# Starting a latent gather in the layer before: rows of the first layer's expert tables fetched during the context's second layer

## The chip, the cores and the metric

The kernel runs on one core of a Trainium2 chip. The metric is the time of one execution in device microseconds. The engines are named as in the profile: PE is the matrix engine (TensorE), DVE the vector engine (VectorE), ACT the scalar engine (ScalarE), POOL the GpSimd engine, SP the queue that issues most loads and stores.

## What is computed

One inference step of a two-layer trunk for two token streams: 128 context tokens (modulated, reading only themselves) and 512 latent tokens (reading the context too). Each layer is a mixer of three branches and then an expert layer (PEER):

```python
x <- LayerNorm(alpha*x + gate1 * W_out( sum_b sigmoid(g_b(h)) * P_b(mixer_b(h)) ))   # gated scan, convolution, attention
x <- LayerNorm(alpha*x + gate2 * PEER(h))
```

```python
q = (xf @ w_pq).reshape(nt, PEER_HEADS, 2, PEER_DQ // 2)
s = jnp.einsum('thpc,hpkc->thpk', q, keys)
s1, i1 = lax.top_k(s[:, :, 0], PEER_TOPK)
s2, i2 = lax.top_k(s[:, :, 1], PEER_TOPK)
...
top_s, top_pos = lax.top_k(cand, PEER_TOPK)
eidx = jnp.take_along_axis(cidx, top_pos, axis=-1)
gate = jax.nn.softmax(top_s, axis=-1)
...
act = jax.nn.gelu(jnp.einsum('td,thkd->thk', xb, u_tab[ib]), approximate=False)
return jnp.einsum('thk,thkd->td', gb * act, v_tab[ib])
```

There are 8 heads of 16 chosen experts, so 128 chosen rows of `u_tab` and 128 of `v_tab` for each token, out of 16384 rows of 1024 numbers each.

## The kernel before

Work is in tiles of 128 tokens: one for the context, four for the latents. The expert layer is done in two ways. For a tile that is **gathered** (the context's one tile, and tile 0 of the latents, in each layer), `peer_gather` fetches for each of the 128 choices one row per token by an indirect DMA on the POOL queue (128 rows of 4 KB, 0.5 MB, into a buffer `grow`), and DVE works it in: a product summed into `gw` for a row of the u table (`gjunk`, L922), and a multiply-add into `gacc` for a row of the v table (L934). After each 16 u rows ACT takes a Gelu of 16 columns. That makes 256 rows a tile. For the other three latent tiles the layer is **dense**: PE multiplies all 128 blocks of 128 experts by the tokens. `u_hidden` loads a block of the u table, splits it on ACT and DVE into a high and a low part (`uH`, `uL`) and makes 24 matmuls of 128x384. Some of the blocks (108 of 128 in the first layer, 64 in the second: `AHEAD`) are done early by `u_ahead`, and their results are stored in DRAM (`sdr`). `gate_map` turns the routing into dense maps (`ob`, `oa`, `stage`, stored to `gdr`). In `peer_dense` each pair of blocks loads its part of the maps (`G`), loads or computes its hidden values (`da`), applies Gelu and map, splits them (`daH`, `daL`), and multiplies by two loaded blocks of the v table (`wraw`, split to `wh`, `wl`) into six accumulators (`acc`): 36 matmuls of 128x512.

The pieces run beside each other through generators. `bg_add(gen, rate)` registers one; each `tick()` in the foreground work advances every registered generator by its rate, and `bg_drain` runs it to its end. Within this program order, the framework's scheduler arranges each engine's queue by when it expects operands and buffers to be ready; a tile whose buffers are all held waits for one to be released. The rates are a hand-set table (`BG`, `RU`, `RG`): `BG[4]` is the rate of the latents' routing (`front`), `RU` that of `u_ahead`, `RG` that of the latents' gather.

The order in the first layer: the context's first layer and the latents' mixer (with the context's gather beside them); then the latents' normalisation, their routing in the background (`routing_keys`: eight projections by `w_pq`, then for each tile and head a score tile and the best 16; `routing_pairs`: the best 16 of the pairs, for four tiles), the second context layer in the foreground (`ctx_front(l + 1)`) and `u_ahead` in the background; then the gate maps of tiles 1 to 3, beside which the gather of tile 0 begins; then the dense stage with the rest of the gather at a rate worked out so that it ends ten ticks early. In the second layer there is no context work left, and the routing's pairs lie beside the gate maps.

Buffers that matter here: `x4`, four slots of 4 KB a partition with the tag `t4k`, which hold in turn the latents' `xlat`, the latents' `VV` and `SG` in the scan, and `uH` and `uL`. `grow` has five buffers in the gate stage and eight (shared with `wraw`) in the dense stage. In the context's scan (`gla_proj`, `gla_core`) `VV` and `SG` have buffers of their own, and `E`, the decay factors of one of seven levels, has two.

```python
    def t4k(shape, name, dt=F32, s=None, p=None):
        if s is not None and s.ctx:
            return p.tile(shape, dt, name=name, bufs=1)
        return x4.tile(shape, dt, tag="t4k", name=name)
```

Of the kernel before, what the change touches and what calls it, by code (L numbers as in the profile page):

```python
# [9 lines left out]
F32 = mybir.dt.float32  # L10
# [33 lines left out]
def kernel(ctx: ExitStack, tc: tile.TileContext, A: dict, O: list):  # L44
# [352 lines left out]
    def gla_proj(s, l, hH, hL, gp, setup, heads):  # L397

        a2, gb, gn, gaT, t4n = setup
        QK = gp.tile([128, 2, 4, 128], F32, name="QK", bufs=1 if s.ctx else 2)  # L400
        VV = t4k([128, 4, DV], "VV", F32, s, gp)
        SG = t4k([128, 4, DV], "SG", F32, s, gp)
        ZB = gp.tile([128, 2, 4, 128], F32, tag="t4", name="ZB", bufs=t4n)
# [24 lines left out]
    def gla_core(s, l, u, gp, t4n, QK, VV, SG, ZB):  # L428
# [25 lines left out]
        for li, m in enumerate(LEVELS):  # L454
            nb = 512 // (2 * m)
            E = gp.tile([128, 2, 512], F32, name="E", bufs=2)
            Ev = E.rearrange("p i (b h m) -> p i b h m", h=2, m=m)
# [332 lines left out]
    def routing_keys(s, l, hH, hL, vals, idxs, qp):  # L790

        for u in range(8):
            keys = qp.tile([128, 2, 128], F32, name="keys", bufs=2)
            nc.sync.dma_start(keys, A["keysT"][l, :, 2 * u:2 * u + 2, :])
            ps = proj_fm(s, hH, hL, w_for(s, A["w_pq"][l, u]))
            qs = []
            for f in range(2):
                q = qp.tile([128, s.T], F32, name="q", bufs=2)
                act(q, ps[f], AF.Copy)
                qs.append(q)  # L800
            for t in range(s.nt):
                p = pb([128, 2, 128])
                for f in range(2):
                    nc.tensor.matmul(p[:, f, :], qs[f][:, t * 128:(t + 1) * 128], keys[:, f, :], start=True, stop=True)
                sc = qp.tile([128, 2, 128], F32, name="sc", bufs=2)
                act(sc, p, AF.Copy)
                for f in range(2):
                    hp = 2 * u + f
                    top16(vals[t][:, hp, :], idxs[t][:, hp, :], sc[:, f, :])
                yield  # L810
# [342 lines left out]
    def run(gen):  # L1153
        for _ in gen:
            pass
# [98 lines left out]
    PL = (5, 5, 5, 2, 0)  # L1254
    BG = (0.55, 2.0, 2.8, 3.622, 0.8)
    FL = (0, 1, 0, 1)
# [3 lines left out]
    OB = ('APDAPADA', 'APDAPADA')  # L1260
    RG = (2.0, 1.056)
    RU = ((0.7, 1.0), (0.84, 0.8))
# [71 lines left out]
    for l in range(DEPTH):  # L1334
# [17 lines left out]
        with pool("e_lat") as ep:  # L1352
# [3 lines left out]
            more = l + 1 < DEPTH  # L1356

            def front(qp):
                yield from routing_keys(Lt, l, hH, hL, vals, idxs, qp)
                if more:  # L1360
                    for t in range(4):
                        yield from routing_pairs(t, vals, idxs, ep, qp, ro)

            ahead = pool("u_t6")
            ucfg.update(p=ahead.__enter__(), n=1, pool_l=PU[0])
            eu = bg_add(u_ahead(l, hH, hL), RU[l][0], PR[0])
            with w_pool(3, 2, PL[2]), pool("ro_lat", 2) as qp:
                with pool("ln_lat2") as lp:
                    run(ln_finish(Lt, 2 * l + 1, ln_rows(lp, 4), True))
                e = bg_add(front(qp), BG[4], PR[5])  # L1370
# [3 lines left out]
            ahead.__exit__(None, None, None)  # L1374
            gout = []
            ucfg["l"] = l
            with pool("g_lat") as gp, pool("u_lat") as up_:
                ucfg.update(p=up_, n=2, pool_l=PU[1 + l])
                with pool("gm") as qp:
# [7 lines left out]
                    pairs(0)  # L1387
                    e = bg_add(peer_gather(Lt, l, 0, ro[0][0], ro[0][1], gp, gout), RG[l], PR[1])
                    pairs(1)
# [6 lines left out]
                with pool("dense") as dp, w_pool(8, 3, PL[3 + l]):  # L1396
                    gcfg.update(p=wcfg["p"], tag="wraw", n=8, m=2)
                    e[1] = (256 + LAG - e[3]) / (256 - AHEAD[l] - 10)
                    peer_dense(Lt, l, hH, hL, dp, e, gout, gp)


# [109 lines left out]
```

## Time and profile before

| | |
|---|---|
| median of 3 runs | 5828.63 us (5822.93 to 5830.19) |
| the profiled execution | 5830.46 us, span 5828.7 us, clock 0.944 |
| busy PE, DVE, ACT, POOL | 89%, 74%, 35%, 46% of the span |
| mean DMA rate | 239 GB/s |

The span is the time from the first to the last instruction of the profiled execution. A busy share is a mean over stages with different limits. The granted clock is TensorE's: 1.00 stands for 2.4 GHz, 0.5 for 1.2 GHz.

### The profile page before, as it was taken

What the parts mean: (1) busy time and instruction counts of PE and PEld (TensorE: products, weight loads), DVE (VectorE), ACT (ScalarE), POOL (GpSimd) and SP (SyncE); (2) the same over time, 40 slices, a digit from 0 to 9 for tenths busy, and PEclk for the clock granted to TensorE, in tenths of its full rate; (3) what the DMA queues carried; (4) which work ended last, traced back from release to release, by engine and by line L of the source; (5) the groups of instructions that cost most, each with busy time, mean ns of one, the idle gap of its engine ahead of it and who ended that gap; (6) DMA issues with size and microseconds to landing.
All of it is one profiled execution on the core that took longest, in us unless ns stands there. A gap on an engine that the chain in (4) does not pass through costs nothing. (4 is left out here: it accounts for less than half of the span.)

```text
span 5828.7 us, 79381 instructions
## 1 busy us (share of the span) xinstructions
PE 5182.8 (89%) x28598; PEld 4504.3 (77%) x28598; DVE 4316.1 (74%) x7923; ACT 2048.9 (35%) x3446; POOL 2681.1 (46%) x2207
## 2 busy tenths in 40 slices
PE   7998799888899998899999787999989778899997
PEld 5887678767788898888777676777777778799876
DVE  3328878878554868887777788788778898777677
ACT  2213334221222125653333333333222356433333
POOL 1215544675210216775444455456752566444322
PEclk9999999999899999999999899999989889999999
DMA  7763356887556557889988533578852667888895
GB/s 279 268 237 114 109 191 220 302 290 255 203 208 240 191 205 270 314 326 321 319 305 312 193 112 125 188 259 296 280 181 93 231 235 258 290 273 278 278 315 207
DMA packets 456714, 1395.14 MB, mean 239 GB/s; under 512 B 42880, under 2 KB 184832, under 8 KB 413312
## 3 DMA queue, kind: packets, MB, share of 16 engines
q1 hardware_dynamic: 303248, 833.73, 40.2%
q0 software_dynamic: 153072, 556.34, 27.9%
q8 instruction: 225, 3.69, 0.2%
q14 instruction: 169, 1.38, 0.1%
HBM read 1275.29 MB, written 114.62 MB: 238 GB/s over the span
## 5 line engine op out<-in xcount | busy, mean ns | idle before, releaser
L917 POOL DMA_INDIRECT grow<-in_peer_v_dram,eidx x512 | 661.8, 1293 | 663.4 <-DVE gacc L934 291.6
L917 POOL DMA_INDIRECT grow<-in_peer_u_dram,eidx x512 | 666.4, 1302 | 567.4 <-DVE gjunk L922 198.3
L934 DVE SCALAR_TENSOR_TENSOR gacc<-grow,gw,gacc 128x1024 f32<-128x1024 f32 x508 | 689.0, 1356 | 91.3 <-DMA grow<-in_peer_v_dram,eidx 85.9
L922 DVE SCALAR_TENSOR_TENSOR gjunk<-grow,gh 128x1024 bf16<-128x1024 f32 x512 | 675.0, 1318 | 74.1 <-DMA grow<-in_peer_u_dram,eidx 65.9
L172 ACT ACTIVATE wh<-wraw 128x1024 fp32r<-128x1024 f32 (+1 forms) x388 | 515.3, 1343 | 540.7 <-PE pa L197 214.5
L174 DVE TENSOR_TENSOR wl<-wraw,wh 128x1408 fp32r<-128x1408 f32 (+2 forms) x388 | 565.9, 1461 | 177.1 <-ACT wh L172 175.6
L196 PE MATMUL acc<-wh,daH 128*128 128x512 f32 x1536 | 615.2, 401 | 60.4 <-ACT daH L110 46.3
L176 POOL TENSOR_TENSOR wl<-wraw,wh 128x640 fp32r<-128x640 f32 (+1 forms) x260 | 375.2, 1445 | 618.7 <-ACT wh L172 599.2
L198 PE MATMUL acc<-wh,daL 128*128 128x512 f32 x1536 | 614.4, 400 | 15.8 <-DVE daL L111 15.7
L197 PE MATMUL acc<-wl,daH 128*128 128x512 f32 x1536 | 610.7, 398 | 0.5 <-DVE wl L174 0.5
L196 PE MATMUL pa<-hH,wh 128*128 128x512 f32 x1312 | 544.3, 415 | 45.0 <-DVE th L746 12.3
L198 PE MATMUL pa<-hH,wl 128*128 128x512 f32 x1312 | 536.5, 410 | 11.7 <-DVE wl L174 11.5
L197 PE MATMUL pa<-hL,wh 128*128 128x512 f32 x1312 | 535.6, 408 | 0.7 <-DVE hL L111 0.7
L196 PE MATMUL po<-hH,uH 128*128 128x384 f32 x1376 | 492.3, 358 | 41.9 <-ACT uH L1014 20.0
L198 PE MATMUL po<-hH,uL 128*128 128x384 f32 x1376 | 478.3, 348 | 28.9 <-DVE uL L1016 28.8
L1014 ACT ACTIVATE uH<-uraw 128x1024 fp32r<-128x1024 f32 x256 | 270.6, 1057 | 590.6 <-PE po L197 201.5
L197 PE MATMUL po<-hL,uH 128*128 128x384 f32 x1376 | 476.1, 346 | 0.0
L196 PEld LDWEIGHTS acc<-wh,daH 128*128 128x128 f32 x1536 | 295.8, 193 | 131.5 <-ACT daH L110 58.4
L1016 DVE TENSOR_TENSOR uL<-uraw,uH 128x1024 fp32r<-128x1024 f32 (+1 forms) x256 | 290.9, 1136 | 115.2 <-ACT uH L1014 108.8
L198 PEld LDWEIGHTS acc<-wh,daL 128*128 128x128 f32 x1536 | 295.5, 192 | 94.1 <-DVE daL L111 32.2
L197 PEld LDWEIGHTS acc<-wl,daH 128*128 128x128 f32 x1536 | 296.4, 193 | 62.0 <-DVE wl L174 1.0
L1063 DVE TENSOR_TENSOR da<-da,G 128x384 f32<-128x384 f32 x256 | 184.1, 747 | 214.3 <-ACT da L1056 208.9
(367 smaller groups left out, 12228.2 us busy)
## 6 DMA issues: line engine op xcount, KB each, us to landing
wraw<-in_w_in_dram SPq DMA_DIRECT2D x168, 1024.0 KB
uraw<-in_u_T_dram SPq DMA_DIRECT2D x256, 512.0 KB
wraw<-in_v_n_dram SPq DMA_DIRECT2D x256, 512.0 KB
wraw<-in_w_mod_dram SPq DMA_DIRECT2D x48, 1024.0 KB
wraw<-in_w_branch_dram SPq DMA_DIRECT2D x48, 1024.0 KB
gdr<-stage SPq DMA_DIRECT2D x24, 2048.0 KB
G<-gdr SPq DMA_DIRECT2D x64, 768.0 KB
sdr<-ust SPq DMA_DIRECT2D x172, 192.0 KB
```

Of the source, the lines that this page charges most:

```text
L172: act(H, raw, AF.Copy)
L174: V.tensor_sub(L[:, :m], raw[:, :m], H[:, :m].bitcast(F32))
L176: nc.gpsimd.tensor_sub(L[:, m:], raw[:, m:], H[:, m:].bitcast(F32))
L196: nc.tensor.matmul(out, aH, bH, start=start, stop=False)
L197: nc.tensor.matmul(out, aH, bL, start=False, stop=False)
L198: nc.tensor.matmul(out, aL, bH, start=False, stop=stop)
L917: nc.gpsimd.indirect_dma_start(out=g, out_offset=None, in_=A[tab + str(l)], in_offset=bass.IndirectOffsetOnAxis(ap=eidx[:, j:j + 1], axis=0))
L922: pin(V.scalar_tensor_tensor(junk, g, 1.0, h, op0=OP.mult, op1=OP.mult, accum_out=w[:, j:j + 1]))
L934: pin(V.scalar_tensor_tensor(acc, g, w[:, j:j + 1], acc, op0=OP.mult, op1=OP.add))
L1014: act(uH, raw, AF.Copy)
L1016: V.tensor_sub(uL[:, :m, :], raw[:, :m, :], uH[:, :m, :].bitcast(F32))
L1063: V.tensor_mul(af, af, G[0][:, :, 2 * (i % 2) + f, :])
```

## The change

The gather of the first layer's tile 0 is registered as soon as that tile's routing is known, inside `front`, which runs beside the second context layer, at 1.6 rows a tick there; before, it was registered after the first call in the gate stage. In the gate stage its rate is 2.0 as before, and in the dense stage the rate is worked out from the rows that remain, as before. Its pool `g_lat` opens earlier, and a pool `g_rows` gives `grow` three buffers in the new place. The routing's rate `BG[4]` goes from 0.8 to 1.2.

Room for this comes from several tiles: in the second context layer `VV` and `SG` use the shared `t4k` slots; `E` has one buffer in both context layers; `keys` has one for the latents; the two `q` of a projection have one buffer each under names of their own (two before, in turn); in the first layer's routing `wh` and `wl` have one buffer and the normalisation's rows two instead of four.

```diff
-        VV = t4k([128, 4, DV], "VV", F32, s, gp)
-        SG = t4k([128, 4, DV], "SG", F32, s, gp)
+        room = None if l else s
+        VV = t4k([128, 4, DV], "VV", F32, room, gp)
+        SG = t4k([128, 4, DV], "SG", F32, room, gp)
...
-            E = gp.tile([128, 2, 512], F32, name="E", bufs=2)
+            E = gp.tile([128, 2, 512], F32, name="E", bufs=1 if s.ctx else 2)
...
-            keys = qp.tile([128, 2, 128], F32, name="keys", bufs=2)
+            keys = qp.tile([128, 2, 128], F32, name="keys", bufs=1 if s.nt > 1 else 2)
...
-                q = qp.tile([128, s.T], F32, name="q", bufs=2)
+                q = qp.tile([128, s.T], F32, name="q%d" % f, bufs=1)
...
-    BG = (0.55, 2.0, 2.8, 3.622, 0.8)
+    BG = (0.55, 2.0, 2.8, 3.622, 1.2)
...
-    RG = (2.0, 1.056)
+    RG = (2.0, 1.056, 1.6)
...
+            def gather(rate):
+                return bg_add(peer_gather(Lt, l, 0, ro[0][0], ro[0][1], gp, gout), rate, PR[1])
+
             def front(qp):
                 yield from routing_keys(Lt, l, hH, hL, vals, idxs, qp)
                 if more:
                     for t in range(4):
                         yield from routing_pairs(t, vals, idxs, ep, qp, ro)
-
+                        if not t:
+                            eg.append(gather(RG[2]))
+
+            eg = []
+            gpool = pool("g_lat")
+            rows = pool("g_rows")
+            if more:
+                gp = gpool.__enter__()
+                gcfg.update(p=rows.__enter__(), tag="grow", n=3, m=1)
...
-            with w_pool(3, 2, PL[2]), pool("ro_lat", 2) as qp:
+            with w_pool(3, 1 if more else 2, PL[2]), pool("ro_lat", 2) as qp:
                 with pool("ln_lat2") as lp:
-                    run(ln_finish(Lt, 2 * l + 1, ln_rows(lp, 4), True))
+                    run(ln_finish(Lt, 2 * l + 1, ln_rows(lp, 2 if more else 4), True))
...
-                    e = bg_add(peer_gather(Lt, l, 0, ro[0][0], ro[0][1], gp, gout), RG[l], PR[1])
+                    if more:
+                        e = eg[0]
+                        e[1] = RG[l]
+                    else:
+                        e = gather(RG[l])
```

Two places in the queues show what moves. The first is POOL in the second context layer, from the first tile's routing products (`oh`) to the first additions of a branch into `mg`. Before:

```order
L848 TENSOR_TENSOR oh<-oh,xf 128x256 x16
L748 TENSOR_TENSOR mg_14094<-mg_14094,th 128x128 x2
L848 TENSOR_TENSOR oh<-oh,xf 128x256 x4
L748 TENSOR_TENSOR mg_14095<-mg_14095,th 128x128 x2
L848 TENSOR_TENSOR oh<-oh,xf 128x256 x12
```

and now:

```order
L849 TENSOR_TENSOR oh<-oh,xf 128x256 x5
L918 DMA grow<-in_peer_u_dram,eidx 128x1024 x13
L575 MEMSET z 128x1
L576 MEMSET z 128x1
L918 DMA grow<-in_peer_u_dram,eidx 128x1024 x15
L849 TENSOR_TENSOR oh<-oh,xf 128x256 x16
L918 DMA grow<-in_peer_u_dram,eidx 128x1024 x4
L918 DMA grow<-in_peer_v_dram,eidx 128x1024 x16
L918 DMA grow<-in_peer_u_dram,eidx 128x1024 x6
L749 TENSOR_TENSOR mg_14363<-mg_14363,th 128x128 x2
L918 DMA grow<-in_peer_u_dram,eidx 128x1024 x7
L749 TENSOR_TENSOR mg_14364<-mg_14364,th 128x128 x2
```

The convolution's last `z`, the second tile's `oh` and the `mg` additions now stand behind gathers, 61 of them ahead of the second `mg`; before, none was among them.

The second place is DVE between the splits of the twenty-second and the twenty-third expert block of `u_ahead`. Before, the convolution stands there:

```order
L576 TENSOR_TENSOR z<-pa,cc 128x128
L579 SCALAR_TENSOR_TENSOR yc<-z,cw,yc 128x128
L580 SCALAR_TENSOR_TENSOR yc<-z,cw,yc 128x128
L576 TENSOR_TENSOR z<-pa,cc 128x128
L579 SCALAR_TENSOR_TENSOR yc<-z,cw,yc 128x128
L580 SCALAR_TENSOR_TENSOR yc<-z,cw,yc 128x128
L174 TENSOR_TENSOR wl<-wraw,wh 128x1408
L584 TENSOR_TENSOR yc<-yc,pa 128x128 x2
L1016 TENSOR_TENSOR uL<-uraw,uH 128x1024
```

and now, in part (the search of the second tile's pairs is `cand`, `top` and `pos`):

```order
L923 SCALAR_TENSOR_TENSOR gjunk,gw<-grow,gh 128x1024
L789 MAX_INDEX pos<-top,cand 128x8
L923 SCALAR_TENSOR_TENSOR gjunk,gw<-grow,gh 128x1024
L824 TENSOR_TENSOR cand<-vals_11287 128x128
L827 TENSOR_SCALAR cand<-vals_11287 128x8
L923 SCALAR_TENSOR_TENSOR gjunk,gw<-grow,gh 128x1024
L785 MAX top<-cand 128x8
L276 TENSOR_TENSOR mT<-pmod,bT 128x16
L786 MAX_INDEX pos<-top,cand 128x8
L277 TENSOR_SCALAR modT_95<-mT 128x16
L787 MATCH_REPLACE cand<-top,cand 128x136
L923 SCALAR_TENSOR_TENSOR gjunk,gw<-grow,gh 128x1024
```

Sixteen gathered rows stand between these two splits, with single small operations between them, and the last projection's `wl`, which stood here, has gone to just behind the seventeenth block.

## Rows read from the trace of the kernel before

**Rows 1.** Part 1 of the page: busy us, share, instructions.

```profile
PE 5182.8 (89%) x28598; PEld 4504.3 (77%) x28598; DVE 4316.1 (74%) x7923; ACT 2048.9 (35%) x3446; POOL 2681.1 (46%) x2207
```

**Rows 2.** Busy time by stretch: us, PE, PEld, DVE, ACT, POOL, PEclk, DMA share, GB/s.

```profile
900.00:1000.00 100.00, 98.52 (x584) 80.90 (x583) 86.68 (x151) 40.36 (x82) 51.20 (x45) 1.00 0.74 242
1496.00:1737.00 241.00, 228.50 (x1429) 197.40 (x1428) 120.20 (x438) 66.32 (x111) 40.42 (x40) 0.96 0.61 215
1737.00:1949.00 212.00, 204.25 (x1433) 183.96 (x1432) 108.64 (x473) 54.82 (x147) 24.98 (x30) 0.99 0.64 224
1949.00:2088.00 139.00, 120.15 (x807) 117.48 (x807) 117.25 (x406) 20.48 (x43) 47.65 (x69) 0.91 0.51 191
...
2204.00:2594.00 390.00, 344.72 (x2094) 336.03 (x2093) 334.32 (x477) 250.12 (x529) 292.65 (x210) 0.93 0.82 299
2594.00:2737.00 143.00, 140.73 (x698) 127.91 (x699) 118.59 (x121) 51.04 (x62) 95.50 (x80) 0.98 0.93 327
2737.00:3201.00 464.00, 422.92 (x1727) 335.51 (x1727) 339.37 (x398) 169.05 (x195) 196.68 (x203) 0.95 0.91 314
```

**Rows 3.** The same for PE's matmuls into `acc` alone: us, busy, PEclk, DMA share.

```profile
2737.00:3201.00 464.00, 422.92 (x1727) 0.95 0.91 314
...
5517.00:5549.00 32.00, 32.00 (x142) 1.00 0.95 325
5549.00:5772.00 223.00, 207.63 (x867) 0.97 0.90 310
```

**Rows 4.** The same for POOL's gather issues into `grow` alone.

```profile
1496.00:2204.00 708.00, 2.03 (x2) 0.97 0.61 214
2204.00:2594.00 390.00, 133.28 (x98) 0.93 0.82 299
...
2737.00:3201.00 464.00, 132.77 (x109) 0.95 0.91 314
3201.00:3272.00 71.00, 6.22 (x5) 0.98 0.60 207
...
5549.00:5772.00 223.00, 57.58 (x41) 0.97 0.90 310
```

**Rows 5.** Who waited for whom, 2700 to 3250: us, times, longest.

```profile
ACT da L1056 <- DMA da<-sdr: 308.4, 52, 11.3
...
PE acc L196 <- ACT daH L110: 33.4, 17, 5.0
```

**Rows 6.** The page's costliest groups: busy us, mean ns, idle before.

```profile
L934 DVE SCALAR_TENSOR_TENSOR gacc<-grow,gw,gacc 128x1024 f32<-128x1024 f32 x508 | 689.0, 1356 | 91.3 <-DMA grow<-in_peer_v_dram,eidx 85.9
L922 DVE SCALAR_TENSOR_TENSOR gjunk<-grow,gh 128x1024 bf16<-128x1024 f32 x512 | 675.0, 1318 | 74.1 <-DMA grow<-in_peer_u_dram,eidx 65.9
...
L1014 ACT ACTIVATE uH<-uraw 128x1024 fp32r<-128x1024 f32 x256 | 270.6, 1057 | 590.6 <-PE po L197 201.5
```

**Rows 7.** Line 917, POOL's gather issues: ns min, median, max.

```profile
L917 POOL DMA_INDIRECT grow<-in_peer_u_dram,eidx x512: 932/1099/2977, 554.9 to 5590.5; - x171
```

**Rows 8.** Timeline at 985: start, us, idle before; an issue and its row's use.

```profile
985.53 1.80 POOL L917 DMA_INDIRECT grow<-in_peer_u_dram,eidx  x1 [0.82 <-DVE den L714]
...
991.61 1.23 DVE L922 SCALAR_TENSOR_TENSOR gjunk<-grow,gh 128x1024 bf16<-128x1024 f32 x1 [0.80 <-DMA grow<-in_peer_u_dram,eidx]
```

**Rows 9.** DVE's groups from 1500 to 2200: busy us, mean ns, idle.

```profile
L1016 DVE TENSOR_TENSOR uL<-uraw,uH 128x1024 fp32r<-128x1024 f32 x55 | 69.5, 1263 | 51.4 <-ACT uH L1014 51.3
L849 DVE TENSOR_REDUCE sel<-oh 128x16 f32<-128x256 f32 x66 | 27.5, 417 | 17.8 <-POOL oh L848 17.6
...
L788 DVE FIND_INDEX8 idxs<-vals,sc 128x8 uint32<-128x128 f32 x80 | 22.1, 285 | 0.0
```

**Rows 10.** Who waited for whom on PE, 1490 to 2204.

```profile
PE pa L363 <- DVE th L746: 13.1, 3, 5.2
```

**Rows 11.** ACT's groups from 550 to 2204: table loads before a Gelu.

```profile
L925 ACT ACT_TABLE_LOAD x5 | 6.4, 1283 | 0.1
```

**Rows 12.** PE's groups from 0 to 400, the first context pass.

```profile
L473 PE MATMUL pb<-E 128*128 128x128 f32 x56 | 7.8, 282 | 1.8 <-POOL E L469 1.1 <-DVE mT L276 0.7
```

More of the change, by code (lines that the diff above doesn't have):

```diff
@@ L1356 @@
             more = l + 1 < DEPTH
+            gout = []
+            gp = None
+            def gather(rate):
+                return bg_add(peer_gather(Lt, l, 0, ro[0][0], ro[0][1], gp, gout), rate, PR[1])
             def front(qp):
@@ L1374 @@
             ahead.__exit__(None, None, None)
-            gout = []
+            if more:
+                rows.__exit__(None, None, None)
+            else:
+                gp = gpool.__enter__()
             ucfg["l"] = l
-            with pool("g_lat") as gp, pool("u_lat") as up_:
+            with pool("u_lat") as up_:
                 ucfg.update(p=up_, n=2, pool_l=PU[1 + l])
@@ L1387 @@
                     pairs(0)
-                    e = bg_add(peer_gather(Lt, l, 0, ro[0][0], ro[0][1], gp, gout), RG[l], PR[1])
+                    if more:
+                        e = eg[0]
+                        e[1] = RG[l]
+                    else:
+                        e = gather(RG[l])
                     pairs(1)
@@ L1399 @@
                     peer_dense(Lt, l, hH, hL, dp, e, gout, gp)
+            gpool.__exit__(None, None, None)
 _OUTS = [((1, 128, 1024), 'float32'), ((1, 512, 1024), 'float32'), ((1, 2, 128, 4, 64), 'float32'),
```

## The prediction

> **What bounds the kernel now.** I read the split into stretches first, then who waits inside each. TensorE is the busiest engine, at 89% of the span [rows 1], so a change pays only where TensorE stands still or runs slowly. Three stretches of the first layer matter. The context's second layer, with the latents' routing beside it, runs from 1496 to 2204; the gate maps from 2204 to 2594; the dense expert stage from 2594 to 3272. The granted clock and the DMA share in the rows tell them apart [rows 2].
>
> Dense stage: I call two expert blocks, 36 matmuls into the accumulators, a pair. From 2737 to 3201 there are 1727 of them, 48 pairs, so 9.67 us a pair [rows 3]. TensorE is busy 422.9 of 464 us at clock 0.95, with DMA at 0.91 and 314 GB/s [rows 2]. The second layer's dense stage has two comparable stretches: 32 us with TensorE always busy, 142 matmuls, 8.11 us a pair at clock 1.00; and 223 us, 867 matmuls, 9.26 us a pair [rows 3]. The slow stretch carries 109 gathered rows, 2.27 a pair; the 9.26 us stretch 41 rows, 1.70 a pair [rows 4]. The reader should see in the waits that ScalarE stands 308 us of 550 for the stored hidden rows (`da<-sdr`) from DRAM, and that TensorE then waits for `daH`, made from them [rows 5]. So loads arrive late while the gather adds 0.5 MB a row to full DMA engines.
>
> Context stretch: TensorE is busy 228.5 of 241 us, then 204.3 of 212, then 120.2 of 139 [rows 2]. No gather runs there (two rows at its end) [rows 4]. VectorE is only half busy until 1949 and 84% busy after, when the latents' pair search is done [rows 2]. TensorE is the bound until 1949; after that both engines are nearly full.
>
> Gate maps: VectorE is busy 334 of 390 us, TensorE 345, DMA 0.82 [rows 2], with 98 gather issues [rows 4]. Neither of the two engines has much room.
>
> **The change, part by part.** By the instruction order, 81 of the 256 rows are issued before the gate maps instead of none; the gate maps keep some 96; the dense stage has 79 left instead of 162, of which 23 (instead of 46) fall in its first ten pairs and 56 in the other 54 pairs, 1.04 a pair.
>
> Dense: the first ten pairs have TensorE busy 140.7 of 143 us already [rows 2], so nothing is won there. For the 48 pairs two bounds. The slope between the stretches with 2.27 and 1.70 rows a pair is (9.67 - 9.26) / 0.57 = 0.72 us a row; at 1.04 rows that gives 9.67 - 1.23 x 0.72 = 8.78, a gain of 0.89 x 48 = 43 us. If the DMA engines stop being full, a pair takes 8.11 us and the gain is 1.56 x 48 = 75 us. I take 55, between them and nearer the slope, because 8.11 was held for 32 us only. The tail after 3201 has 5 rows [rows 4] and gains nothing.
>
> Context stretch, first part (to 1737): the front's rate goes from 0.8 to 1.2, so before the seventeenth expert block seven of the latents' eight projections stand, not five, and 28 score tiles, not 19 (counted over the order). Two projections are 96 matmuls of 128x512; at 32/142 = 0.225 us each [rows 3] that is 22 us. This part is TensorE-bound at 228.5/241 = 95%, so 22/0.95 = 23 us longer. A score tile is ten searches on VectorE of 0.28 us [rows 9] and six small value loads, some 3.3 us, so the nine are 30 us; VectorE, busy 120 of 241 us [rows 2], has the room.
>
> Second part (1737 to 2088, 351 us): TensorE's 324.4 us lose those 22, VectorE's 225.9 lose 30 and gain 81 rows x 1.34 us (1318 and 1356 ns) [rows 6] = 108. Their sum goes from 550 to 606. How much of both engines can lie side by side is read from rows: 1.57 us of work per us over the 351 now, 1.71 in the stretch from 1949, and 1.85 in 900 to 1000, where the context's first gather runs beside the latents' mixer [rows 2]. 606 divided by these is 386, 354 and 328: a change of +35, +3 or -23. I take +12, near the middle one, since the same two engines run nearly full there. Sum of the context stretch: 23 + 12 = +35, with ends 0 and +58.
>
> What the 81 rows need beside VectorE: 81 POOL issues at a median of 1.1 us [rows 7], 89 us on an engine that is busy 25 of 212 and 48 of 139 us here [rows 2], and 42 MB, 135 us of the DMA engines at the dense stage's 314 GB/s, where their share is 0.51 to 0.64 [rows 2]. Both are covered by the projections. Six more table loads on ScalarE, for the gather's Gelu, cost 6 x 1.28 = 8 us [rows 11] of an engine busy 54.8 of 212 and 20.5 of 139 [rows 2]; covered. By the Trainium skill, "ScalarE: Activation LUTs", section "What ACT_TABLE_LOAD costs", a switch also drains for about 1.4 us; with it the six would be 16 us, still covered, and the sum would stay.
>
> Single buffers. `E` in the context's scan: TensorE waited 1.8 us for it in the first context pass [rows 12]; with one buffer each of seven levels could expose its own chain of about 3 us, so 0 to 20 us. I take 2 for the first pass (other projections lie between) and keep the second pass within the +35. `VV` and `SG` of the second context pass now hold two of the four `t4k` slots, so until the scan ends one expert block's `uH` and `uL` fill the rest: 1.06 + 1.26 us [rows 6, 9] would be bare for twelve blocks, 28 us, but the order puts 16 context matmuls or a whole projection between two blocks. Zero, with 28 kept for the range. `wh`/`wl`, `keys`, `q`, two `lnrow`: each has over 10 us of other matmuls between uses; zero.
>
> Gate maps: the same 96 rows. The stretch loses the last routing of the latents on VectorE, some 8 us of work, but waits for the same maps. I take -2, with 8 either way.
>
> Sum: -55 + 35 + 2 - 2 = -20. The profiled execution took 5830.5 us (span 5828.7), 1.8 above the median of the three runs. 5830.5 - 20 - 1.8 = 5809 us.
>
> **The rivals.**
> *Late rows hold VectorE (slower).* `grow` has three buffers in the new place. A row lands about 6.1 us after its issue: issued at 985.53, used at 991.61 on a DMA wait [rows 8]. Three rows therefore need about 6.1 + 1.3 = 7.4 us; the order gives each three 4.0 us of their own work and 4 to 5 us of other work, 8.0 to 9.3, so at that landing time it fits. If rows land in 9.5 us, as full DMA engines would have it, each of 27 threes stops VectorE for some 2 us: 54 us. POOL is in order, so behind a gather that waits for a buffer stand the `z` memsets, the `oh` products and the `mg` adds; the adds free `th`, and TensorE already lost 13 us to `th` [rows 10]. It decides from 0.75 us a three (20 us). Time 5809 + 54 = 5863. For it: the first 25 rows stand nearly back to back. Against: DMA is at 0.51 to 0.64 there [rows 2]. By the Trainium skill, "DMA: Bandwidth & Descriptors", section "Anatomy of one DMA — SWDGE (gpsimd) path", a transfer takes 2.0 us and its bytes at 436 GB/s, which I estimate as 3.2 us for one row; the rival would be empty by that. The row shows twice as much, and I go by the row.
>
> *POOL and VectorE lock each other out (no change).* A gather issue took 932 ns at least and 2977 at most [rows 7], so something delays it; if each of the 64 `oh` products, for which VectorE already stood 17.6 us [rows 9], waits half a gather operation (0.65 us) and half shows, 21 us go: 5830. By the Trainium skill, "SBUF — State Buffer", section "Who interferes with whom", a VectorE instruction with two SBUF inputs contends with a POOL instruction that reads SBUF, and both gather operations have two. Against: POOL is idle most of the time.
>
> *The dense stage isn't relieved (slower).* If `da<-sdr` is late for its prefetch of one pair and not for the traffic, only some 10 us are won: 5809 + 45 = 5854. Against: the time a pair follows the rows a pair in three stretches.
>
> *The gather costs nothing in the context stretch (faster).* With the sum at 1.85 both parts cancel: 0 instead of +35, 5774.
>
> **How the numbers follow.** Forecast 0.48, late rows 0.22, lock 0.10, dense not relieved 0.08, free gather 0.12. The likeliest alone: 5790 to 5830. With the other cases and the single buffers' 28 us, 5764 to 5863 leaves about 2 in 10 out. A measurement here tells 0.2%, 12 us, from no change. The forecast gives 0.43 faster and 0.05 same, the free gather 0.12 faster, the lock 0.09 same and 0.01 slower, the two slower rivals 0.27 slower and 0.03 same: 0.55, 0.17, 0.28.
>
> **What would show it.** Right: the accumulators' pairs at 8.4 to 8.7 us with about one row each and DMA at 0.8; a context stretch 20 to 50 us longer with VectorE near 85% after the seventeenth block; a gate stage of the same length. Wrong: VectorE's idle time before `gjunk` and `gacc` from DMA in the context stretch, tens of us (late rows); POOL's `oh` products lengthened (lock); ScalarE still 300 us behind `sdr` at one row a pair (not relieved).

## The result, and the profile after

The changed kernel took 5879.55 us (median of 4 runs, 5875.85 to 5884.82), the kernel before beside it 5826.24 us: a ratio of 1.0092, with a 95% interval of 1.0074 to 1.0109. It is slower by 53 us, where 20 us less was forecast. The profiled execution after took 5875.85 us (span 5874.1, 45.4 more than before). Of all executions in this document one, of e12 (6043 us at a granted clock of 0.82), was slow and is left out of its row below.

I cut the span of both kernels at the same events: the first matmul of the first expert block, the gate maps' first `ob`, the first and the last matmul into `acc`. Busy time by stretch after (us, PE, PEld, DVE, ACT, POOL, PEclk, DMA share, GB/s), first the context stretch whole, then its four parts, then the gate maps and the dense stage:

```profile
1511.75:2325.09 813.34, 704.53 (x4517) 644.91 (x4515) 526.48 (x1760) 183.20 (x371) 217.94 (x235) 0.94 0.67 239
...
1511.75:1766.46 254.71, 248.76 (x1563) 215.68 (x1562) 146.33 (x610) 73.38 (x123) 36.86 (x33) 0.99 0.59 207
1766.46:2010.00 243.54, 195.38 (x1309) 177.55 (x1308) 175.85 (x549) 52.43 (x141) 88.39 (x98) 0.89 0.78 284
2010.00:2178.00 168.00, 126.97 (x810) 122.91 (x809) 114.54 (x289) 22.64 (x44) 73.31 (x85) 0.87 0.76 278
2178.00:2325.00 147.00, 133.36 (x841) 128.72 (x839) 89.67 (x314) 34.76 (x63) 19.38 (x21) 0.99 0.52 177
...
2325.09:2713.55 388.46, 331.43 (x2022) 326.13 (x2022) 319.23 (x430) 247.85 (x524) 299.30 (x203) 0.93 0.84 301
2713.55:2850.00 136.45, 136.45 (x692) 124.27 (x692) 85.64 (x94) 48.05 (x59) 67.95 (x53) 1.00 0.76 255
2850.00:3258.00 408.00, 394.78 (x1706) 321.36 (x1705) 264.73 (x308) 166.11 (x191) 120.74 (x148) 0.99 0.83 281
```

| | before | after | measured | forecast |
|---|---|---|---|---|
| first expert block begins | 1496.3 | 1511.8 | +15.5 | +2 |
| context stretch, from there to the first `ob` | 708.2 | 813.3 | +105.1 | +35 |
| gate maps, to the first `acc` | 389.4 | 388.5 | -0.9 | -2 |
| dense stage of the first layer | 678.2 | 613.5 | -64.7 | -55 |
| the rest | 2556.6 | 2547.0 | -9.6 | 0 |

The gate maps and the dense stage came out near their size; the first expert block began 13 us later than forecast, and the context stretch cost three times its forecast. The second and third part show it [rows 2]: with rows there, TensorE's busy share is 80% and 76% (96% and 86% before), the clock 0.89 and 0.87 (0.99 and 0.91), and DMA 0.78 and 0.76 in place of 0.64 and 0.51. VectorE, which I expected near 85%, is at 72% and 68%: it stands still too. The fourth part, with one gather issue, is nearer to before: TensorE is busy 91% of it at clock 0.99, 98% at 1.00 from 2088 to 2204 before.

Who waited for whom from 1511 to 2325 (us, times, longest), and behind it the first of these lines in the kernel before (1496 to 2204):

```profile
ACT uH L1015 <- DMA uraw<-in_u_T_dram: 148.4, 20, 17.6
...
DVE gjunk L923 <- DMA grow<-in_peer_u_dram,eidx: 51.2, 27, 5.9
...
DVE gacc L935 <- DMA grow<-in_peer_v_dram,eidx: 30.7, 17, 5.9
```

```profile
ACT uH L1014 <- DMA uraw<-in_u_T_dram: 75.4, 17, 14.3
```

VectorE stood 82 us for rows, and ScalarE's wait for expert blocks (`uraw`) doubled from 75 us. A stretch of VectorE's timeline (start, us, idle before) shows VectorE's wait from close by:

```profile
1905.41 1.22 DVE L923 SCALAR_TENSOR_TENSOR gjunk<-grow,gh 128x1024 bf16<-128x1024 f32 x1 [1.25 <-DMA grow<-in_peer_u_dram,eidx]
...
1906.76 0.29 DVE L785 MAX8 top<-cand 128x8 f32<-128x136 f32 x1
1906.97 0.14 DVE L694 SCALAR_TENSOR_TENSOR nm<-mx,nsink 128x1 f32<-128x1 f32 x1
1910.43 1.23 DVE L923 SCALAR_TENSOR_TENSOR gjunk<-grow,gh 128x1024 bf16<-128x1024 f32 x1 [3.32 <-DMA grow<-in_peer_u_dram,eidx]
...
1912.94 1.23 DVE L923 SCALAR_TENSOR_TENSOR gjunk<-grow,gh 128x1024 bf16<-128x1024 f32 x1 [0.99 <-DMA grow<-in_peer_u_dram,eidx]
```

Small operations of the search and the attention fill a microsecond between two rows, and then the engine stands for the next one. From 1890 to 2135 a row landed 7.0 us after its issue at the median, where I had used 6.1 [rows 8]:

```profile
DMA to landing us min/median/max: 4.3/7.0/10.4
```

By the Trainium skill, "Perfetto Trace Analysis", section "DMA Instruction — SWDGE (GPSIMD)", the end of such an issue's record is the end of its descriptors, not of the data; the trace agrees, with 0.94 us for an issue's record and 7.0 us to the landing.

In the dense stage, from 2850 to 3258, the same views: PE's matmuls into `acc`, POOL's gather issues, and the two waits of [rows 5] (those from 2713 on):

```profile
2850.00:3258.00 408.00, 394.78 (x1706) 0.99 0.83 281
```

```profile
2850.00:3258.00 408.00, 68.73 (x54) 0.99 0.83 281
```

```profile
ACT da L1057 <- DMA da<-sdr: 233.0, 47, 11.3
...
PE acc L196 <- ACT daH L110: 5.2, 4, 2.1
```

1706 matmuls are 47.4 pairs, so 8.61 us a pair in place of 9.67, with 1.14 rows a pair in place of 2.27. ScalarE still waits for `sdr`, but in time: TensorE's wait for `daH` falls from 33.4 to 5.2 us.

### The profile page after: what moved, and what is told of

Same layout as the page of the kernel before. It is cut to its first block, busy times and chain, and to the rows that moved or that the text cites. A ratio compares the mean times of both kernels' runs of the same rounds, so it can differ in the third digit from the quotient of the medians.

```text
span 5874.1 us, 79301 instructions
## 1 busy us (share of the span) xinstructions
PE 5166.9 (88%) x28598; PEld 4506.6 (77%) x28598; DVE 4294.9 (73%) x7923; ACT 2054.7 (35%) x3452; POOL 2686.6 (46%) x2207
## 5 line engine op out<-in xcount | busy, mean ns | idle before, releaser
L196 PEld LDWEIGHTS pa<-hH,wh 128*128 128x128 f32 x1312 | 254.2, 194 | 110.6 <-DVE th L747 13.9
```

Of the source, the lines that this page charges most:

```text
L196: nc.tensor.matmul(out, aH, bH, start=start, stop=False)
```

## The experiments

The theory after the result was **late rows** (VectorE is in order and stands for rows that three buffers cannot bring in time), with the rivals **buffers and rate** and **VectorE's work**; later **traffic** and **POOL in order**. The stages are cut as above, each from one profiled execution. Runs of one kernel lay within 7 to 36 us of each other; the profiled executions of the rate alone (5792) and of the last version (5789) are the fastest of theirs, that of e8 (5813) the slowest. So a difference of stages under 10 us says little. Each ratio is against runs of the kernel before taken beside it, whose median lay between 5820.1 and 5826.2 us; I compare kernels of different series by their ratios.

| kernel | median us | ratio, 95% interval | first block | context stretch | gate maps | dense |
|---|---|---|---|---|---|---|
| before | 5826.2 | | 1496 | 708 | 389 | 678 |
| the change | 5879.6 | 1.0092 [1.0074, 1.0109] | 1512 | 813 | 388 | 613 |
| e1 gather late | 5831.6 | 1.001 [1.0001, 1.002] | 1499 | 694 | 398 | 676 |
| e2 rate alone | 5806.7 | 0.9969 [0.9956, 0.9983] | 1488 | 688 | 389 | 679 |
| e3 rate back | 5885.9 | 1.0108 [1.0083, 1.0133] | 1485 | 812 | 381 | 646 |
| e4 no fetch | 5794.7 | 0.9951 [0.9935, 0.9967] | 1512 | 721 | 391 | 618 |
| e5 rows unread | 5858.5 | 1.0058 [1.0037, 1.0079] | 1507 | 786 | 395 | 619 |
| e6 two weight buffers | 5897.2 | 1.0115 [1.0082, 1.0148] | 1500 | 825 | 393 | 619 |
| e6 the same, five row buffers | 5883.1 | 1.0093 [1.0067, 1.012] | 1505 | 813 | 394 | 619 |
| e7 half the rows | 5832.2 | 1.0014 [1.0001, 1.0026] | 1511 | 761 | 366 | 649 |
| e8 no fetch, bound | 5801.5 | 0.9965 [0.9953, 0.9978] | 1509 | 727 | 401 | 617 |
| e9 unread, bound | 5864.8 | 1.0086 [1.0063, 1.011] | 1506 | 797 | 386 | 616 |
| e10 short rows | 5858.6 | 1.0062 [1.0043, 1.0081] | 1506 | 790 | 390 | 615 |
| e11 DRAM copies | 5859.5 | 1.0079 [1.0055, 1.0103] | 1501 | 795 | 390 | 612 |
| e12 short rows, POOL freed | 5835.3 | 1.0024 [1.0009, 1.004] | 1507 | 760 | 395 | 619 |
| e13 copies, two `uraw` | 5853.6 | 1.0058 [1.0039, 1.0077] | 1504 | 777 | 392 | 616 |
| e14 the change, POOL freed | 5868.8 | 1.0082 [1.0063, 1.0101] | 1508 | 795 | 394 | 617 |
| e15 gather late, two `uraw` | 5837.9 | 1.003 [1.0017, 1.0043] | 1498 | 717 | 386 | 679 |
| e16 rate 1.6 alone | 5808.9 | 0.9974 [0.9958, 0.9989] | 1489 | 691 | 388 | 685 |
| e17 half the rows, POOL freed | 5807.8 | 0.9977 [0.9968, 0.9986] | 1503 | 734 | 362 | 642 |

**e1, the gather late.** In the changed kernel:

```diff
-                        if not t:
-                            eg.append(gather(RG[2]))
...
-                    if more:
-                        e = eg[0]
-                        e[1] = RG[l]
-                    else:
-                        e = gather(RG[l])
+                    e = gather(RG[l])
```

> The changed kernel with all its single buffers and its routing rate of 1.2, but with the gather registered in the gate stage as before. Theory 'late rows' (the stretch's excess comes from gathered rows that three buffers cannot bring in time: VectorE stood 82 us for them in the changed kernel): the context stretch falls from 813 us to 720 to 740, the start stays about 15 us late, the dense stage is back at 675 to 680, so 5826 + 15 + 20 = about 5860. Rival 'buffers and rate' (the single buffers, the shared t4k slots and the faster routing make the excess, the rows only fill gaps): the context stretch stays above 780 us and the dense gain is lost, so 5920 or more.

**e2, the rate alone.** In the kernel before, `BG[4]` from 0.8 to 1.2.

> The kernel before with the routing's rate at 1.2 in place of 0.8 and nothing else. The prediction's own sum had two projections moved ahead of the seventeenth expert block and paid back behind it: by it the stretch's first part grows by 23 us and its second shrinks by as much, so within 10 us of 5826. Rival 'the rate makes the excess': 20 us or more above, with the context stretch at 730 or more in place of 708.

**e3, the rate back.** In the changed kernel, `BG[4]` from 1.2 to 0.8.

> The changed kernel with the routing's rate back at 0.8: the first tile's choices are known later, and by the order 52 rows are issued ahead of the gate maps in place of 81. 'Late rows': VectorE's idle time for rows falls about with their number, from 82 to about 50 us, and the context stretch by about 30 to 40; the dense stage gives up about a third of its 65, so about 5865. 'Buffers': the stretch hardly moves and the dense gain shrinks, 5890 to 5900. 'Rate': the stretch comes down by 50 or more, 5830 to 5850.

**e4, no fetch.** In the changed kernel, with what the 81 rows contribute left out of the result:

```diff
         def fetch(tab, j):
+            if gcfg["n"] == 3:
+                return h
             g = row()
```

> The changed kernel, but its early rows are not fetched: VectorE makes the same products and multiply-adds on a tile that is already there, so its work is kept and the waits for rows, POOL's issues and the traffic of those 81 rows are gone. 'Late rows': the context stretch falls from 813 by 60 to 90 us to some 730 to 750 and the dense stage keeps its gain, so 5790 to 5820. Rival 'VectorE's work' (the 108 us of added VectorE operations themselves push the projections and expert blocks apart): the stretch stays above 780 and the time above 5845.

The context stretch of e1 and of e2, each as one window (columns as above):

```profile
1499.00:2192.99 693.99, 653.92 (x4351) 601.25 (x4352) 412.74 (x1540) 168.77 (x350) 117.05 (x144) 0.98 0.62 216
```

```profile
1487.77:2175.93 688.16, 656.54 (x4424) 602.95 (x4423) 419.08 (x1598) 172.16 (x356) 125.27 (x153) 0.98 0.64 223
```

"Buffers and rate" falls: without the early rows all the buffers and the rate together cost 7 us, and the stretch is shorter than before. Both expectations of e1 were too long, though: 694 us and 5832, where "late rows" had 720 to 740 and 5860. The rate alone is a gain, 0.9969, and 20 us of the stretch; neither expectation of e2 had that. So the two parts of the 7 us are a gain of 18 from the rate and a loss of 25 from the buffers (e1 against e2: 1.001 and 0.9969, with intervals apart). e4 puts the price on the fetching: the same 4517 matmuls take 721 us in place of 813. e3 came out near what "buffers" had expected, which e1 rules out: 52 rows, the first issued at 1947 in place of 1832, make the stretch 104 us longer than the kernel before at the same rate (708), and 81 rows make it 119 longer than e1 (694). The price is not in proportion to the number of rows there.

**e5, rows unread.** In the changed kernel, `fetch` issues the row as before and then returns the resident tile in the early place (`return h if gcfg["n"] == 3 else g`).

> The changed kernel, whose early rows are fetched as before into the three buffers but not read: VectorE makes its products and multiply-adds on a tile that is already there. The 42 MB and POOL's 81 issues are kept, and only VectorE's wait for rows is taken away. Theory 'VectorE waits' (VectorE is in order, and what TensorE needs stands behind a row that has not landed): near the run without fetches, a context stretch of 715 to 745 us and 5790 to 5815 in all. Rival 'traffic' (the rows delay the loads of expert blocks and projections) or 'POOL' (issues that wait for a buffer hold the oh and mg behind them): the stretch stays above 780 us and the time above 5850.

**e6, more row buffers**, and its control with two weight buffers alone:

```diff
-                gcfg.update(p=rows.__enter__(), tag="grow", n=3, m=1)
+                gcfg.update(p=rows.__enter__(), tag="grow", n=5, m=1)
...
-            with w_pool(3, 1 if more else 2, PL[2]), pool("ro_lat", 2) as qp:
+            with w_pool(2 if more else 3, 1 if more else 2, PL[2]), pool("ro_lat", 2) as qp:
```

> Control for the next run: the changed kernel with two buffers in place of three for the weights (wraw) of the context stretch, which makes room for two more row buffers, and no other difference. The weights' loads lose some lead: 0 to 20 us above the changed kernel, 5880 to 5900.

> The same two weight buffers, and five row buffers (grow) in the early place in place of three. 'VectorE waits': a row is asked for two rows earlier, VectorE's idle time for rows in the context stretch falls from 82 to below 40 us, and the time is 30 to 60 us below the control, some 5830 to 5860. 'Traffic' or 'POOL': within 15 us of the control.

**e7, half the rows.** In the changed kernel, `RG[2]` from 1.6 to 0.8.

> The changed kernel with the early gather at 0.8 rows a tick in place of 1.6; by the order 40 rows are issued ahead of the gate maps in place of 81. 'VectorE waits': a row that stands twice as far from the next mostly lands in time, VectorE waits 20 us or less for rows, the context stretch is 715 to 750, the dense stage gives up half of its 65, and the time is 5800 to 5830. Rival 'a price for each row' (in proportion to rows, whatever their spacing): half of the 92 us that fetching costs, a stretch of 760 to 770 and 5840 to 5860.

My theory did not stand. Without VectorE's waits the stretch was still 786 us, not 715 to 745. VectorE's waits for rows in the control, and with five row buffers:

```profile
DVE gjunk L923 <- DMA grow<-in_peer_u_dram,eidx: 50.5, 25, 4.5
DVE gacc L935 <- DMA grow<-in_peer_v_dram,eidx: 29.2, 13, 4.3
```

```profile
DVE gacc L935 <- DMA grow<-in_peer_v_dram,eidx: 10.1, 7, 4.0
DVE gjunk L923 <- DMA grow<-in_peer_u_dram,eidx: 9.8, 12, 1.9
```

80 us of waiting became 20, and the stretch went only from 825 to 813, with 52 more matmuls in it (4465 and 4517); TensorE's idle time there fell from 116 to 93 us. The waits are real, but taking them away uncovers others. With half the rows the stretch is 761 us, what the rival "a price for each row" had expected (760 to 770), and 67 us above e1; the whole is 8 us below its range, by a shorter gate stage.

e4 and e5 had a fault of their own. Their resident tile is ready early, and 49 of the 81 operations moved ahead of the seventeenth expert block. The next four bind them to the routing with one operation of 128x128 behind `gh`:

```diff
         V.tensor_add(h, h, sh)
+        if gcfg["n"] == 3:
+            V.scalar_tensor_tensor(h[:, :128], gate, 0.0, h[:, :128], op0=OP.mult, op1=OP.add)
```

**e8** is e4 with this line, **e9** is e5 with it.

> The run without fetches again, with VectorE's products bound behind the routing: one small operation makes the resident tile depend on the first tile's gates, so that the 81 operations stand in VectorE's queue where the changed kernel has them (in the run without fetches 49 of them had moved ahead of the seventeenth expert block). Theory 'fetching' (waits, POOL's issues or traffic cost the stretch): 715 to 745 us from the first expert block to the gate maps, and 5790 to 5820 in all. Rival 'VectorE's work in that place': 770 us or more, 5840 or more.

> The same binding, and the rows are fetched into the three buffers and not read. Against the run without fetches it adds POOL's 81 issues and 42 MB; against the changed kernel it takes away only VectorE's wait for rows. 'VectorE waits': within 20 us of the run without fetches. 'Traffic' or 'POOL': the stretch is 770 to 800 us, 5845 to 5865 in all, as in the unbound run.

**e10, short rows:** as e9, from a view of the table with 16 numbers a row.

```diff
+            if gcfg["n"] == 3:
+                nc.gpsimd.indirect_dma_start(out=g[:, :16], out_offset=None, in_=A[tab + str(l)].rearrange("n (a b) -> (n a) b", b=16),
+                                             in_offset=bass.IndirectOffsetOnAxis(ap=eidx[:, j:j + 1], axis=0))
+                return h
```

> The same as the unread rows, but each row has 16 numbers in place of 1024: POOL makes the same 81 issues for three buffers, and the traffic is a sixty-fourth. 'POOL' (issues that wait for a buffer or delay the oh and mg behind them): within 20 us of the unread rows. 'Traffic': near the run without fetches, a stretch of 715 to 750 us and 5790 to 5825.

**e11, DRAM copies:** as e8, with a copy by SP for each row (`last` is VectorE's operation on the row before).

```diff
+            if gcfg["n"] == 3:
+                r = slice(j * 128, j * 128 + 128)
+                behind(nc.sync.dma_start(gcopy[tab][r], A[tab + str(l)][r]), last[0])
+                return h
```

> The same as the run without fetches, but SP issues 81 copies of 0.5 MB from the tables to another place in DRAM, ordered behind the operations that would use the rows: traffic of that size without POOL, without row buffers and without anyone who waits for it. 'Traffic': the stretch is 30 to 70 us longer than without fetches, 5830 to 5870. 'POOL': within 15 us of the run without fetches.

The context stretch of e8, e10 and e11, in this order:

```profile
1509.27:2236.16 726.89, 680.73 (x4517) 625.00 (x4515) 521.18 (x1760) 184.61 (x371) 129.53 (x154) 0.97 0.59 209
```

```profile
1506.40:2295.96 789.56, 688.39 (x4517) 630.91 (x4515) 520.29 (x1760) 184.07 (x371) 220.43 (x236) 0.93 0.55 194
```

```profile
1500.65:2295.16 794.51, 706.01 (x4517) 642.42 (x4515) 521.58 (x1760) 186.62 (x371) 130.71 (x154) 0.95 0.68 244
```

All have the matmuls and the VectorE work of the changed kernel. Without fetching the stretch takes 727 us; POOL's issues alone make it 790, traffic alone 795, both without a reader 797, the changed kernel 813. "POOL" had expected e10 long and e11 short, "traffic" the reverse; both are long, and with both together nothing is added. The prices, 63, 68 and VectorE's last 16, do not add up to 86: they overlap. The ratios of the whole say the same with 56 us for e10, 66 for e11, 70 for e9 and 74 for the change, each less e8; between e9 and the change they show no difference (1.0086 and 1.0092). And e9 is not quite the change without VectorE's waits: a buffer that nobody reads is free as soon as its row has landed, so POOL goes by landings there and not by VectorE's use.

In e10 the long waits are few. The first two lines are DVE's and the third PE's:

```profile
DVE sel L850 <- POOL oh L849: 62.1, 54, 40.5
...
DVE yc L580 <- POOL z L576: 20.5, 1, 20.5
...
PE pa L363 <- DVE mg L747: 34.8, 1, 34.8
```

From its timeline, POOL ahead of the longest of these, and DVE behind it:

```profile
1960.14 0.94 POOL L921 DMA_INDIRECT grow<-in_peer_v_dram,eidx  x1 [0.30 <-issue]
1961.39 0.94 POOL L921 DMA_INDIRECT grow<-in_peer_u_dram,eidx  x1 [0.30 <-issue]
1962.36 0.73 POOL L849 TENSOR_TENSOR oh<-oh,xf 128x256 f32<-128x256 f32 x1
```

```profile
1963.12 0.42 DVE L850 TENSOR_REDUCE sel<-oh 128x16 f32<-128x256 f32 x1 [40.54 <-POOL oh L849]
...
1967.57 0.47 DVE L747 SCALAR_TENSOR_TENSOR mg<-th,pa 128x128 f32<-128x128 f32 x2
```

POOL issues one row every 1.25 us in a block; `oh` stands behind it, `sel` waits 40.5 us for `oh`, `mg` stands behind `sel`, and TensorE waits for `mg`. In the changed kernel, where a row's use holds the next issue back, such blocks don't form (`sel` waits 22 us in all, 18 before [rows 9]), so e10's 63 us are not POOL's share there; e14 comes nearer to that.

In e11 nobody waits for the copies, and POOL has no issues. The waits there are for expert blocks; those of e8 behind it:

```profile
ACT uH L1023 <- DMA uraw<-in_u_T_dram: 123.5, 27, 16.6
...
PE po L198 <- DVE uL L1025: 38.6, 18, 9.0
```

```profile
ACT uH L1019 <- DMA uraw<-in_u_T_dram: 66.2, 12, 9.2
...
PE po L198 <- DVE uL L1021: 9.0, 6, 3.2
```

By the Trainium skill, "DMA: Bandwidth & Descriptors", section "Issuing engines are not separate DMA queues", transfers that different engines start run on the same 16 DMA engines and interleave. The runs are in line with it: with copies that SP asked for, expert blocks came late as they do with rows that POOL asks for (a wait of 123.5 us here, 148.4 in the changed kernel). But SP's queue, which also issues the blocks' loads, gets 81 issues of 0.5 us with the copies, some 40 us; e11 does not separate these from the bytes.

**e12** is e10, and **e14** the changed kernel, with `oh`, `z` and `mg` on VectorE in the early place:

```diff
-            nc.gpsimd.memset(z[:, 0:1], 0.0)
+            P = V if gcfg.get("n") == 3 else nc.gpsimd
+            P.memset(z[:, 0:1], 0.0)
...
-                    (nc.gpsimd if FL[1] else V).tensor_add(m, m, th[f])
+                    (V if gcfg.get("n") == 3 else nc.gpsimd).tensor_add(m, m, th[f])
...
-                nc.gpsimd.tensor_mul(oh, oh, xf[:, h, q, None, :].to_broadcast([128, 16, 16]))
+                (V if gcfg["n"] == 3 else nc.gpsimd).tensor_mul(oh, oh, xf[:, h, q, None, :].to_broadcast([128, 16, 16]))
```

> The run with short rows again, but in the stretch with the early gather POOL has the row issues alone: the routing's 'oh' products, the convolution's 'z' memsets and the 'mg' adds go to VectorE. Theory 'POOL in order' (a short row costs by holding these three behind row issues): the stretch falls from 790 us to 735 to 765, no lower because VectorE takes over 64 products and 16 adds, some 30 us; 5805 to 5835 in all. Rival 'the issues themselves' (POOL's issue or its instruction traffic slows TensorE or VectorE wherever it stands): 780 us or more.

> The changed kernel with oh, z and mg on VectorE in the stretch with the early gather, rows fetched and used as in the changed kernel. POOL's share alone is taken away. If the causes add up, the stretch loses some 60 us less VectorE's 30: 770 to 785 and 5840 to 5855. If they overlap (late rows and late loads hold the same engines at the same time), less than 15 us is won: 800 to 815 and 5865 to 5885.

**e13** is e11, and **e15** is e1 without row buffers, with two `uraw` and `ust` in the first layer's context stretch (`ucfg.update(..., n=1 if l else 2, ...)`).

> The run with DRAM copies again, with two buffers in place of one for an expert block's load (uraw) and its result (ust) in the context stretch, and two row buffers, which the copies don't use, in place of three. Theory 'late expert blocks' (the traffic costs because a block's load can only start when the block before it is split, and then takes longer): the stretch falls from 795 us to 730 to 755 and ScalarE's wait for uraw from 124 to below 70 us. Rival 'the engines are full' (the bytes themselves, whatever the lead): 780 us or more.

> A version: routing at 1.2, the single buffers of the change, the gather late as before, and the room of the row buffers given to a second uraw and ust in the context stretch. ScalarE's wait for uraw there falls below 30 us. If expert blocks' loads bound the stretch without rows too, it falls from 694 to about 670 and the whole to 5790 to 5805; if not, it stays at 685 to 695, near 5830 (the run with the gather late) or 5806 (the rate alone).

e12 fell where "POOL in order" had put it: 760 us, and 22 us of the whole. That does not show the theory, for the 33 us that e12 still has above e8 are less than a single standstill in it, with `oh`, `z` and `mg` no longer on POOL. TensorE's longest wait in the stretch, SP's longest (both us, times, longest), and ScalarE's first operation behind it:

```profile
PE pb L267 <- DMA wraw<-in_w_mod_dram: 53.1, 1, 53.1
```

```profile
SPq L1020 <- DMA grow<-in_peer_v_dram,eidx: 53.4, 1, 53.4
```

```profile
1970.33 0.28 ACT L725 ACTIVATE yatT<-pt 128x128 f32<-128x128 f32 x1 [56.27 <-issue]
```

From 1914 to 1967 POOL issues 43 short rows close behind one another. TensorE waits for a weight load that stands in SP's queue behind the load of the next expert block, and ScalarE for nothing that the trace shows. The operations that read the block before had ended by 1914, so why SP's load started at 1967.7 is open. The rival "the issues themselves" is therefore not excluded for short rows. In the changed kernel, where rows are used, TensorE's longest pause is 10.7 us, so a standstill of this kind is not among its costs.

In the changed kernel the edit of e12 takes 18 us from the stretch (e14), between the two expectations, and the intervals of the whole (1.0082 and 1.0092) overlap. e13 is between its two theories too: the stretch falls by 18 us and ScalarE's wait for `uraw` from 124 to 99, which fits a single buffer that carries a part of the traffic's price, though the intervals of the whole (1.0079 and 1.0058) overlap. What carries the other 50 us is not settled. In e15 ScalarE's wait for `uraw` fell below 30 us as expected (16, from 41 in e1), but the stretch of 717 us was a miss: it holds 166 more matmuls than e1's (4517 and 4351), and in the whole a second `uraw` without rows wins nothing.

**e16** is the kernel before with `BG[4]` at 1.6, **e17** is e7 with the edit of e14.

> A version: the kernel before with the routing's rate at 1.6 and nothing else (1.2 gave 18 us). If the gain comes from the pairs' search on VectorE having moved out of the stretch's crowded end, a still earlier search keeps it or adds a little: 5795 to 5810. If 1.2 was only a lucky order, it is lost: 5815 to 5830.

> A version: the changed kernel with half as many early rows (0.8 a tick), and oh, z and mg on VectorE in the stretch. The half rate gave 5832 and a stretch of 761 us; the freed POOL took 18 us from the stretch at the full rate. If that adds here, 5812 to 5822, still above the rate alone; if half the rows leave POOL's queue no cost, 5828 to 5836.

Both are faster than before, by 0.3% and 0.2%, and as fast as the rate alone. e16 is where a lasting gain had been expected (5795 to 5810), so by that expectation 1.2 was not a lucky order; e17 came out below its 5812 to 5822. e17 is the early gather at its best here, with 41 rows: against e1 the stretch is 40 us longer, the dense stage 34 shorter and the gate maps 36 shorter. It is faster than the change by some 70 us, but not measurably better than one number in the kernel before. That the gate maps take 362 and 366 us in the two kernels with half the rows, against 381 to 401 in all others, I did not expect and have not explained, and without it these stages of e17 would be no shorter than e1's.

## Why the prediction was wrong

*Dense stage, -55: right.* 65 us, inside the ends of 43 and 75, with 8.61 us a pair (8.4 to 8.7 forecast) at DMA 0.83. Over all kernels the stage follows the rows that are left in it: 676 to 685 us with 156 gather issues there, 642 to 649 with 105 to 116, 612 to 619 with 75 or 76, so some 0.8 us a row, near the slope of 0.72. The sum of waits behind `sdr` was no measure of it; that they stopped reaching TensorE was.

*Gate maps, -2: right* in the changed kernel (-0.9).

*First context pass, +2: right in its term, wrong in the stage.* At 617 us, with the first context pass behind them, the same VectorE operations of the two kernels are 1.6 us apart, so the single `E` cost what I took. The first expert block came 15.5 us late for another reason: 9.0 us of it are TensorE's wait for the scores' `q`, queued on ScalarE behind a `uH` that waited for `uraw`. In kernels with the same buffers this start lay between 1485 and 1512, so it is a matter of the order.

*Single buffers, 0 with 28 in the range: mis-sized.* e1 against e2 has 6 us more in the stretch, but 25 more in the whole. The profiled executions put 11 before the first expert block and 9 in the gate maps, near the limit of what they can tell; which buffer costs it was not measured.

*The rate:* my own sums gave +23 in the first part and, without the rows, 351 - 498/1.57 = 34 less in the second, so -11; e2 measured -20 in the stretch and -18 in all. Its gain was in the working, but the text showed only its sum with the rows.

*VectorE's 81 rows:* the working gave +12 where it had -34 without them, so +46. e8 less e1 measured +33, of which 27 us are TensorE's own busy time, for 166 more matmuls (some seven expert blocks) that moved into the stretch. e15, with the same 4517 matmuls and no rows, takes 717 us, so VectorE's work itself is worth some 10.

*What the 81 rows need beside VectorE: this step failed.* I had written "Both are covered by the projections", of 89 us of POOL issues and 42 MB, because POOL's busy share and the DMA share [rows 2] left room. Their size was right (POOL's gather issues and the bytes are in the trace as counted); the price was 86 us of the stretch (813 less 727) and 74 of the whole (1.0092 less 0.9965) in place of 0. Of it 63 are idle time of TensorE (109 in place of 46) and 24 the same 4517 matmuls at a granted clock of 0.94 in place of 0.97. A mean share of 0.6 said nothing of a block's load that is already the last thing ScalarE waits for: [rows 5] had shown that pattern for `sdr` at 0.91, and here it appeared at 0.78.

*The rival "late rows" named the sign and nearly the time (5863; measured 5880), and its waits were there:* 82 us on VectorE, 54 forecast. It had taken its landing time of 9.5 us from no row; rows landed in 7.0 at the median and 10.4 at most. But the waits are not what sets the end: with them taken away, the stretch lost 16 us (e9), or 12 with five buffers (e6), and the intervals of the whole overlap in both. Copies alone are enough for 68 of the 86 and freeing POOL gives 18 of the stretch, so the prices hide one another; how much of the 86 each cause has when all are there stays open. The "lock" did not appear: an `oh` product on POOL took 821 ns at the mean in place of 831. It was hardly tried, though: one of the 80 ran beside a gather operation of VectorE. "Dense not relieved" and "gather free" are refuted by the dense stage and by e8.

Without the fetching (e8) the change would have won 0.35%, 20 us, which is just the forecast. That is partly luck: the buffers' 25 us, put at nothing, are made up by 7 more from the rate than the working had (18 for 11), 13 less for VectorE's rows (33 for 46) and 6 more from e8's dense stage (61 for 55). The fetching is the only error of its size.

## What to carry to other kernels

Before transfers are moved into a stretch, look at which loads an engine there waits for already, not at the mean DMA share: here a share of 0.61 hid a wait of 75 us for one load's single buffer, and the wait doubled. When several waits lie over each other, taking one away buys little, and each of them alone can look like the whole cause: measure "none of them" and "each alone", and look into the trace of each, as one can bring a standstill of its own. Undo a change piece by piece: here one number in a table was worth 18 us, and the rest of the change cost some 70.

## What the runs showed of the hardware

Rows of 64 bytes (e10) occupy POOL like rows of 4 KB: 0.94 us an issue at the median, and at the closest 1.24 us from one to the next with either size. Copies of 0.5 MB within DRAM made the stretch as long as rows that nobody reads did (795 and 797 us). Beside 43 short rows that POOL issued in 53 us (e12), with 7 GB/s on the DMA engines, TensorE, ScalarE and SP stood still, and the trace does not say why. TensorE's stalls were paid twice: where it stood for a fifth to a quarter of the time, its granted clock was 0.89 and 0.87 (a mean over its two levels, 1.2 and 2.4 GHz), and the same matmuls took 24 us longer in the whole stretch.
